# Hybrid GLA and differential-attention layer: an earlier split of the forget gate's weights, later stores of operand tiles, another spread of set units

## The chip, the cores and the metric

One core of a Trainium2 chip runs the kernel. The metric is the device time of one execution in microseconds; the time of a kernel is the median over its runs.

## The reference

One decoder layer over 256 tokens with 2048 features, in fp32. A normalised input goes through one wide projection; its columns feed two token mixers, whose outputs are merged by gates and projected once more:

```
h = rmsnorm(x, pre_norm_g);  proj = h @ w_in
a_q, a_k, a_v, a_g, a_lr, b_q, b_k, b_v, b_g, m_a, m_b = split(proj)
gk  = log_sigmoid(a_lr @ gla_gk_w2 + gla_gk_b) / 16          # forget gate
o_a = rmsnorm(gla_chunked(a_q, a_k, a_v, gk)) * silu(a_g);   y_a = o_a @ w_branch_a
o_b = rmsnorm(diff_attention(b_q, b_k, b_v, lam)) * (1 - lam_init) * silu(b_g)
y_b = o_b @ w_branch_b
merged = sigmoid(m_a) * y_a + sigmoid(m_b) * y_b
x = x + rmsnorm(merged @ w_out, post_norm_g)
```

`a_lr` has 16 columns, and `gla_gk_w2` is 16 x 1024. The weights are some 250 MB and are read once; the work is matmuls of 256 tokens against them.

## The kernel before

**Products.** Each fp32 product is made from rounded parts: a value is split into `hi` (a copy to the type fp32r) and `lo` (the rest), and hi x hi, hi x lo and lo x hi are summed. Weights come from DRAM in tiles of 128 x 2048 (1 MB, `raw`, three buffers). Half a tile is a *unit*. For each unit ACT copies it to `hi` (L297), DVE subtracts to get `lo` (L298), and PE multiplies (`token_major`, L457): eight matmuls of 512 columns with `hi`, four with `lo`. `hi` and `lo` have three buffers each, so ACT's copy for a step waits until PE is through with the step three before.

**Set units.** Five pairs of column groups (`SETS`) are computed by a scheme of seven products in place of eight. A product (p1, q3, p5, p2, q6, q7, p4) has four units; that makes 140 *set units*, six matmuls each (L656), whose `hi` and `lo` come from L258 and L259. Their weights are sums: tiles called `chain` are loaded by POOL DMAs (L212 plain, L210 with accumulation in the transfer); p2 needs a plain load `raw_s`, issued by SP (L252), which DVE also adds to a chain tile (L228). The other operand is a sum of parts of x, kept in tiles `square` (s1, n2, s4, n7, a hi and a lo each). They are made once; `store_squares` (called at L847, POOL DMAs at L620) writes all eight to DRAM, from where later sets read them back (`start_sets`, L632).

**Order.** `schedule()` writes the list of steps by hand: ordinary units by key, with set units put between. `mixed(n, *keys)` takes the next n set units and spreads them evenly over the units of these keys. The keys around the change are m12 and m13 (merge gates), y00 to y03 (first branch product: y_a in four groups of 512 columns, 8 units each) and y10 to y13 (second branch product), then o0 to o3. Loads and splits of a step are written down four steps before its matmuls. A scheduler then orders the instructions by priority and its own estimates, unless they are wrapped in `keep_in_program_order`; each engine runs its own list in order.

**Reads back.** The operands of the branch products, `oah` and `oal` for y0, `obh` and `obl` for y1, lie in DRAM and are read back by eight SP DMAs of 512 KB (`fetch`, L723, kept in program order), written down just ahead of y00 and of y10. SP also issues all loads of `raw` (L276), and a load waits on SP until its buffer is free.

**Forget gate.** Small jobs run in the background, one turn at a time, as generators that `pump()` steps. `forget_gate` transposes `lr` on PE (bank `bg`), splits it into `lrt`, splits `w2` into `w_s` (ACT L518, DVE L520) by way of `w2h` (ACT L519), and in its next turns multiplies them (PE L528).

Of the kernel before, what the change touches and what calls it, by code (L numbers as in the profile page):

```python
# [7 lines left out]
F32R = mybir.dt.float32r  # L8
BF16 = mybir.dt.bfloat16
U8 = mybir.dt.uint8  # L10
AF = mybir.ActivationFunctionType
ALU = mybir.AluOpType
AX = mybir.AxisListType

P = 128
# [15 lines left out]
def chunk_plan():  # L31

    plan = []
    at = 0
    for g, n in enumerate(VG):
        if g == 0:
            plan.append(("v0", "two", "w_in", [(6144, RANK), (2048, 2 * n - RANK)]))
            at = 2 * n - RANK
        elif g > 1:
            plan.append((f"v{g}", "tok", "w_in", [(2048 + at, n)]))  # L40
            at += n
    for hf in range(2):
        for name, base in (("k", 1024), ("q", 0)):
            for c in range(4):
                plan.append((f"{name}{hf}{c}", "chan", "w_in", [(base + 512 * hf + P * c, P)]))
    for g in range(4):
        plan.append((f"ag{g}", "tok", "w_in", [(4096 + 512 * g, 512)]))
    o = 6144 + RANK

    def heads(g):  # L50
        plan.append((f"dv{g}", "tok", "w_in", [(o + 4096 + 512 * g, 512)]))
        plan.append((f"bg{g}", "tok", "w_in", [(o + 6144 + 512 * g, 512)]))
        for pair in range(2):
            for n, name in enumerate(("dq", "dk")):
                for c in (2 * pair, 2 * pair + 1):
                    plan.append((f"{name}{g}{c}", "chan", "w_in", [(o + 2048 * n + 512 * g + P * c, P)]))

    def gate(br, g):
        plan.append((f"m{br}{g}", "tok", "w_in", [(o + 8192 + 2048 * br + 512 * g, 512)]))

    def branch(br, g):
        plan.append((f"y{br}{g}", "tok", ("w_branch_a", "w_branch_b")[br], [(512 * g, 512)]))

    for g in range(4):
        heads(g)
    for br, g in ((1, 2), (1, 3), (1, 0), (1, 1), (0, 0), (0, 1), (0, 2), (0, 3)):
        gate(br, g)
    for br in range(2):
        for g in range(4):
            branch(br, g)  # L70
    for g in range(4):
        plan.append((f"o{g}", "tok", "w_out", [(512 * g, 512)]))
    return plan


def units(kind):
    return 2 * KT // ROWS[kind]


def schedule():  # L80

    kinds = {key: kind for key, kind, _, _ in chunk_plan()}
    steps = []
    blocks = [(i, n) for i in range(len(SETS)) for n in range(SLOTS * 4)]

    def regular(*keys):
        steps.extend((key, n) for key in keys for n in range(units(kinds[key])))

    def mixed(n, *keys):
        at = len(steps)  # L90
        regular(*keys)
        r = steps[at:]
        del steps[at:]
        for i, step in enumerate(r):
            steps.extend(blocks[: (i + 1) * n // len(r) - i * n // len(r)])
            del blocks[: (i + 1) * n // len(r) - i * n // len(r)]
            steps.append(step)

    def channels(g):
        return [key for key in kinds if key[:2] in ("dq", "dk") and key[2] == str(g)]  # L100

    order = [key for key, _, _, _ in chunk_plan()]
    def alone(n):
        steps.extend(blocks[:n])
        del blocks[:n]

    regular(*order[: order.index("v4")])
    mixed(SLOTS * 4, *order[order.index("v4") : order.index("ag0")])
    regular(*order[order.index("ag0") : order.index("dq10")])
    mixed(18, *channels(1))  # L110
    mixed(18, *channels(2))
    mixed(18, *channels(3))
    mixed(16, "m12", "m13")
    mixed(32, *(f"y0{g}" for g in range(4)))
    mixed(10, "y10", "y11")
    regular("y12", "y13", *(f"o{g}" for g in range(4)))
    assert not blocks
    return steps
# [26 lines left out]
def hybrid_kernel(ctx: ExitStack, tc, xt, xn, preg, postg, w, w2, gkb, glag, lamv, diffg, ident_d, causal_d, lmask_d, out):  # L145
    nc = tc.nc
    pe, act, dve, pool, sp = nc.tensor, nc.scalar, nc.vector, nc.gpsimd, nc.sync
# [10 lines left out]
    def u(shape, name, dtype=F32):  # L158
        count[0] += 1
        return big.tile(shape, dtype, tag="u", name=f"{name}_{count[0]}")  # L160

    def sm(shape, name, dtype=F32, bufs=2):
        count[0] += 1
        return small.tile(shape, dtype, tag=name, name=f"{name}_{count[0]}", bufs=bufs)

    def t2(shape, name):
        count[0] += 1
        return small.tile(shape, F32, tag="t2", name=f"{name}_{count[0]}", bufs=8)

    def ps(tag):  # L170
        count[0] += 1
        return psum.tile([P, 512], F32, tag="bank", name=f"{tag}_{count[0]}")
# [5 lines left out]
    def f32(ap):  # L178
        return ap.bitcast(F32)


    steps = schedule()
    kinds, sizes, begins = {}, {}, {}
    off = 0
# [164 lines left out]
    w2_raw = u([P, 1024], "w2_raw")  # L349
    w2_s = u([P, 1024], "w2_s", F32R)  # L350
# [152 lines left out]
    act.activation(ones_r, ones, AF.Copy)  # L503

    def forget_gate():
        bank = ps("bg")
        for b in range(2):
            pe.transpose(bank[:, P * b : P * b + P], lr[:, b, :], ident)
        top = t2([P, 512], "lrh").bitcast(F32R)
        lrt = sm([P, S], "lrt", F32R, bufs=1)  # L510
        act.activation(top[:, :S], bank[:, :S], AF.Copy)
        for i in (0, 64):
            act.activation(lrt[i : i + 32, :], bank[i : i + 32, :S], AF.Copy)
            r = slice(i + 32, i + 64)
            dve.tensor_tensor(out=lrt[r, :], in0=bank[r, :S], in1=f32(top[r, :S]), op=ALU.subtract)
        top = u([P, 1024], "w2h", F32R)
        r = slice(64, P)
        act.activation(w2_s[:64, :], w2_raw[:64, :], AF.Copy)  # L518
        act.activation(top[r, :], w2_raw[r, :], AF.Copy)  # L519
        dve.tensor_tensor(out=w2_s[r, :], in0=w2_raw[r, :], in1=f32(top[r, :]), op=ALU.subtract)  # L520
        yield
        for hf in range(2):
            for c in range(2):
                bank = ps("bg")
                for i in range(2):
                    ct = 4 * hf + 2 * c + i
                    o = bank[:, S * i : S * i + S]
                    pe.matmul(o, w2_s[:, P * ct : P * ct + P], lrt, start=True, stop=True)  # L528
                for i in range(2):
                    ct = 4 * hf + 2 * c + i  # L530
                    act.activation(gp[hf][:, :, 2 * c + i, :], bank[:, S * i : S * i + S].rearrange("p (b t) -> p b t", b=2), AF.Identity, bias=gkb_s[:, ct : ct + 1])
            yield
        e = [u([P, 1024], "e") for _ in range(2)]
        z = [t.rearrange("p b c t -> p (b c t)") for t in gp]
        for hf in range(2):
            act.activation(e[hf], z[hf], AF.Abs)
            yield
            act.activation(e[hf], e[hf], AF.Exp, scale=-1.0)
            yield
        for hf in range(2):  # L540
            act.activation(e[hf], e[hf], AF.Ln, bias=1.0)
        for hf in range(2):
            yield
            dve.scalar_tensor_tensor(out=z[hf], in0=z[hf], scalar=0.0, in1=e[hf], op0=ALU.min, op1=ALU.subtract)
        done.add("gate")
# [71 lines left out]
    def store_squares():  # L617
        for name, far in parts_far.items():
            for t, src in zip(far, parts[name]):
                pool.dma_start(t, f32(src))  # L620

    def start_sets():
        n = started[0]
# [112 lines left out]
    tasks.append(late())  # L736
    tasks.append(operands)
    tasks.append(forget_gate())
    start = 2 * VG[0] - RANK
    for g, n in enumerate(VG[2:]):  # L740
# [92 lines left out]
    for hf in range(2):  # L833
        ts = {}
        for name in ("k", "q"):
            ts[name] = u([P, 2, 4, P], name)
            for c in range(4):
                o, o2 = (t.rearrange("p (b t) -> p b t", b=2) for t in channel_major(f"{name}{hf}{c}"))
                bc = rstd_bc.rearrange("p (b t) -> p b t", b=2)
                t = ts[name][:, :, c, :]  # L840
# [4 lines left out]
                pump(1)  # L845
        tasks.append(gla_scores(hf, ts["q"], ts["k"]))
    store_squares()  # L847


# [44 lines left out]
    for g in range(4):  # L894
# [6 lines left out]
        t = u([P, 2, 512], "ua")  # L901
# [207 lines left out]
    for g in range(4):  # L1109
        banks = token_major(f"y0{g}", 512, a_ops)  # L1110
        for b in range(2):
            t = t2([P, 512], "part")
# [49 lines left out]
    for g in range(4):  # L1162
# [8 lines left out]
        for b in range(2):  # L1171
            t = both[g][:, b, :]
# [9 lines left out]
    for b in range(2):  # L1182
        xres.append([])
        for i in range(2):
            t = u([P, 1024], "xres")
# [16 lines left out]
    def subtotal(b, parts):  # L1202
        r = sm([P, 1], "or", bufs=2)
        dve.tensor_reduce(out=r, in_=ssq[:, b, :parts], op=ALU.add, axis=AX.X)
        dve.tensor_scalar(out=r, in0=r, scalar1=1.0 / D, scalar2=EPS, op0=ALU.mult, op1=ALU.add)
        return r
# [30 lines left out]
    for c in range(2):  # L1237
# [6 lines left out]
        if c == 0:  # L1244
            square(1, bank[:, :256], 256, 3)
            gain(1, bank[:, :256], 1536, 256)
            r = subtotal(1, 4)
# [61 lines left out]
```

## Time and profile before

| | |
|---|---|
| runs | 1126.16 us median of 3 (1125.39 to 1126.97) |
| the profiled execution | 1127.69 us, its span 1125.9 us |
| mean granted TensorE clock | 0.994 |
| PE busy | 1108.4 us, 98% of the span, 5578 matmuls |
| DVE, ACT, POOL busy | 819.3, 679.9, 137.1 us |
| DMA | 274.56 MB, mean 244 GB/s |
| PE's longest waits | 3.5 us for `w_s` (L520), 2.0 us for a `lo` (L298) |

The span runs from the first to the last instruction. A timeline row has the start, the duration, engine and line, then output and inputs by the program's names; in brackets stands the idle time before it and what ended it. SPq is the queue of SyncE, which issues DMAs; how long a transfer took is read from its issue to its landing. A window row gives busy time and count of PE, PEld, DVE, ACT and POOL, then the granted clock, the share of the DMA engines and GB/s.

### The profile page before, as it was taken

The page shows a single profiled execution, that of the slowest core. Times are in us where ns is not written, and L with a number is a line of the kernel's source. Part 1 is how long each engine was busy: PE and PEld are TensorE (multiplying, and loading weights), DVE is VectorE, ACT ScalarE, POOL GpSimd, SP SyncE. Part 2 cuts the span into 40 slices and gives each one's busy share as a digit, 9 for nine tenths or more (in the row PEclk, how much of TensorE's full clock was granted, in tenths as well). Part 3 has the DMA queues.
Part 4 walks back from the last instruction along what each step waited for, and adds up shares of the span by engine and source line. Part 5 has one row for each costly group of instructions (what it writes and reads, how often), then busy time and mean ns, then how long its engine had stood idle before and what let it go on. Part 6 is the DMA issues. An engine that isn't in the chain of part 4 may idle for free. (4 is left out here: it accounts for less than half of the span.)

```text
span 1125.9 us, 15164 instructions
## 1 busy us (share of the span) xinstructions
PE 1108.4 (98%) x5578; PEld 954.0 (85%) x5578; DVE 819.3 (73%) x1151; ACT 679.9 (60%) x1004; POOL 137.1 (12%) x209
## 2 busy tenths in 40 slices
PE   9999999999999999999999999999999999999997
PEld 9989888888888888888888888888788888888886
DVE  6786769986677567658888878878676767585554
ACT  7767555654555457656777778775455555534451
POOL 0131100000001021212212312121112100000000
PEclk9998999999999999999999999999999999999999
DMA  8799764556565484989787989779889777588562
GB/s 310 263 375 351 231 186 157 208 185 248 179 257 208 166 310 167 393 208 249 227 277 215 242 254 243 229 216 261 333 300 256 200 300 247 180 342 309 188 211 75
DMA packets 55371, 274.56 MB, mean 244 GB/s; under 512 B 6848, under 2 KB 7488, under 8 KB 36608
## 3 DMA queue, kind: packets, MB, share of 16 engines
q1 hardware_dynamic: 33392, 195.97, 48.2%
q0 software_dynamic: 21184, 76.56, 25.4%
q10 hardware_dynamic: 720, 1.06, 0.3%
q8 instruction: 44, 0.72, 0.2%
q14 instruction: 31, 0.25, 0.1%
HBM read 249.44 MB, written 24.12 MB: 243 GB/s over the span
## 5 line engine op out<-in xcount | busy, mean ns | idle before, releaser
L457 PE MATMUL mm<-hi,xs 128*128 128x512 f32 (+2 forms) x896 | 216.8, 383 | 0.6 <-ACT hi L297 0.6
L478 PE MATMUL mm<-xs,hi 128*128 128x512 f32 x768 | 197.6, 391 | 0.0
L259 DVE TENSOR_TENSOR lo<-chain,hi 128x1024 fp32r<-128x1024 f32 x120 | 146.7, 1224 | 68.6 <-ACT hi L258 68.0
L258 ACT ACTIVATE hi<-chain 128x1024 fp32r<-128x1024 f32 x120 | 127.1, 1060 | 107.5 <-PE mm L457 46.7
L457 PEld LDWEIGHTS mm<-hi,xs 128*128 128x128 f32 x896 | 167.8, 190 | 25.8 <-ACT hi L297 1.1
L478 PEld LDWEIGHTS mm<-xs,hi 128*128 128x128 f32 x768 | 142.7, 188 | 27.3
L457 PE MATMUL mm<-lo,xs 128*128 128x512 f32 (+2 forms) x448 | 117.0, 380 | 0.0
L480 PEld LDWEIGHTS mm<-xs,lo 128*128 128x128 f32 x768 | 104.8, 190 | 7.5
L480 PE MATMUL mm<-xs,lo 128*128 128x256 f32 x768 | 107.1, 282 | 0.0
L298 DVE TENSOR_TENSOR lo<-raw_y,hi 128x1024 fp32r<-128x1024 f32 x64 | 78.1, 1223 | 37.5 <-ACT hi L297 37.3
L297 ACT ACTIVATE hi<-raw_y 128x1024 fp32r<-128x1024 f32 x64 | 67.7, 1062 | 57.1 <-PE mm L457 32.5
L457 PEld LDWEIGHTS mm<-lo,xs 128*128 128x128 f32 x448 | 84.7, 190 | 13.1 <-DVE lo L298 0.3
L656 PE MATMUL set<-hi,square 128*128 128x512 f32 x320 | 87.6, 396 | 0.0
L210 POOL DMA_DIRECT2D chain<-in_w_dram x56 | 48.8, 882 | 194.7 <-DVE lo L259 109.7
L656 PEld LDWEIGHTS set<-hi,square 128*128 128x128 f32 x320 | 58.7, 190 | 10.2
L656 PE MATMUL set<-hi,xs 128*128 128x512 f32 x240 | 65.6, 394 | 0.0
L297 ACT ACTIVATE hi<-raw_ag 128x1024 fp32r<-128x1024 f32 x32 | 33.9, 1061 | 39.9 <-PE mm L457 35.8
L298 DVE TENSOR_TENSOR lo<-raw_ag,hi 128x1024 fp32r<-128x1024 f32 x32 | 39.1, 1223 | 21.4 <-ACT hi L297 21.2
L457 PE MATMUL mm<-hi,obh 128*128 128x512 f32 x128 | 50.0, 391 | 0.8 <-ACT hi L297 0.8
L656 PEld LDWEIGHTS set<-hi,xs 128*128 128x128 f32 x240 | 43.8, 190 | 7.4
L298 DVE TENSOR_TENSOR lo<-raw_o,hi 128x1024 fp32r<-128x1024 f32 x25 | 30.6, 1225 | 26.8 <-ACT hi L297 26.6
L457 PE MATMUL mm<-hi,oah 128*128 128x512 f32 x128 | 49.9, 390 | 0.0
(273 smaller groups left out, 2069.0 us busy)
## 6 DMA issues: line engine op xcount, KB each, us to landing
chain<-in_w_dram POOLq DMA_DIRECT2D x96, 512.0 KB, 8.0
raw_y<-in_w_dram SPq DMA_DIRECT2D x32, 1024.0 KB, 6.3
raw_ag<-in_w_dram SPq DMA_DIRECT2D x16, 1024.0 KB, 4.8
raw_dq<-in_w_dram SPq DMA_DIRECT2D x16, 1024.0 KB, 5.4
raw_dk<-in_w_dram SPq DMA_DIRECT2D x16, 1024.0 KB, 7.4
raw_o<-in_w_dram SPq DMA_DIRECT2D x16, 1024.0 KB, 4.9
raw_v<-in_w_dram SPq DMA_DIRECT2D x15, 832.0 KB, 6.8
raw_s<-in_w_dram SPq DMA_DIRECT2D x10, 1024.0 KB, 8.2
```

The source lines that it names most:

```text
L210: pool.dma_start(dst, src, accum_op=ALU.add)
L258: act.activation(hi_t, raw, AF.Copy)
L259: dve.tensor_tensor(out=lo_t, in0=raw, in1=f32(hi_t), op=ALU.subtract)
L297: act.activation(hi_t[:, a:b], r, AF.Copy)
L298: dve.tensor_tensor(out=lo_t[:, a:b], in0=r, in1=f32(hi_t[:, a:b]), op=ALU.subtract)
L457: i = pe.matmul(banks[g][b][:, :n], a[part][:, P * b : P * b + P], w[:, c : c + n], start=first, stop=last)
L478: i = pe.matmul(o, hi[:, c], x_pair(kt), start=kt == 0, stop=kt == KT - 1)
L480: i = pe.matmul(o[:, :S], lo[:, c], x_ops(kt)[0], start=False, stop=False)
L656: i = pe.matmul(bank, a[part], wt[:, 512 * j : 512 * j + 512], start=go, stop=end, skip_group_check=not first)
```

## The change

1. `forget_gate`: the split of w2 goes ahead of the transposes and has a turn of its own.
2. `store_squares`: the eight stores are kept in program order, so behind what is written before them.
3. `schedule`: m12 and m13 take 14 set units (16 before); y00 takes 4 and y01 to y03 take 28 (the four groups shared 32); y10 and y11 take 12 (10).

```diff
@@ schedule
-    mixed(16, "m12", "m13")
-    mixed(32, *(f"y0{g}" for g in range(4)))
-    mixed(10, "y10", "y11")
+    mixed(14, "m12", "m13")
+    mixed(4, "y00")
+    mixed(28, *(f"y0{g}" for g in range(1, 4)))
+    mixed(12, "y10", "y11")
@@ forget_gate
     def forget_gate():
+        top = u([P, 1024], "w2h", F32R)
+        r = slice(64, P)
+        act.activation(w2_s[:64, :], w2_raw[:64, :], AF.Copy)
+        act.activation(top[r, :], w2_raw[r, :], AF.Copy)
+        dve.tensor_tensor(out=w2_s[r, :], in0=w2_raw[r, :], in1=f32(top[r, :]), op=ALU.subtract)
+        yield
         bank = ps("bg")
...
-        top = u([P, 1024], "w2h", F32R)
-        r = slice(64, P)
-        act.activation(w2_s[:64, :], w2_raw[:64, :], AF.Copy)
-        act.activation(top[r, :], w2_raw[r, :], AF.Copy)
-        dve.tensor_tensor(out=w2_s[r, :], in0=w2_raw[r, :], in1=f32(top[r, :]), op=ALU.subtract)
         yield
@@ store_squares
-                pool.dma_start(t, f32(src))
+                tc.keep_in_program_order(pool.dma_start(t, f32(src)))
```

In what follows y00.2 is unit 2 of the key y00, and p5.1 is unit 1 of product p5. Around the start of y00 the list of steps was: q3.3 m13.1 p5.0 m13.2 p5.1 m13.3 p5.2 m13.4 p5.3 m13.5 q6.0 m13.6 q6.1 m13.7 q6.2 y00.0 q6.3 y00.1 q7.0. It is now: q3.3 m13.3 p5.0 m13.4 p5.1 m13.5 p5.2 m13.6 p5.3 m13.7 y00.0 q6.0 y00.1 y00.2 q6.1 y00.3 y00.4 q6.2.

Three places in the engines' lists follow. First SP at the start of y00; a name like raw_y00_2 is the load of units 2 and 3 of y00, and oah and oal are the reads back. Before:

```order
L276 DMA raw_m13_6_7286<-in_w_dram 128x2048
L276 DMA raw_y00_0_7343<-in_w_dram 128x2048
L723 DMA oah_660_7393<-oah_far_184_2311 128x1024
L723 DMA oal_664_7397<-oal_far_188_2315 128x1024
L723 DMA oah_661_7394<-oah_far_185_2312 128x1024
L723 DMA oal_665_7398<-oal_far_189_2316 128x1024
```

After:

```order
L277 DMA raw_m13_6_7263<-in_w_dram 128x2048
L277 DMA raw_y00_0_7309<-in_w_dram 128x2048
L277 DMA raw_y00_2_7350<-in_w_dram 128x2048
L725 DMA oah_660_7374<-oah_far_184_2311 128x1024
L725 DMA oal_664_7378<-oal_far_188_2315 128x1024
L725 DMA oah_661_7375<-oah_far_185_2312 128x1024
```

raw_y00_2, which stood behind the eight reads back, now stands ahead of them. The load raw_s for p2 (raw_s3_20) stood between the loads raw_y00_4 and raw_y00_6 and now stands behind raw_y01_2. On PE the number of set matmuls ahead of the first matmul with oah goes from 594 to 576, which is three set units of six.

Second, SP at the start of y10, with obh and obl as the reads back. Before:

```order
L276 DMA raw_y10_0_8305<-in_w_dram 128x2048
L276 DMA raw_y10_2_8343<-in_w_dram 128x2048
L723 DMA obh_698_8367<-obh_far_244_3018 128x1024
L723 DMA obl_702_8371<-obl_far_248_3022 128x1024
L723 DMA obh_699_8368<-obh_far_245_3019 128x1024
```

After:

```order
L277 DMA raw_y10_0_8281<-in_w_dram 128x2048
L277 DMA raw_y10_2_8370<-in_w_dram 128x2048
L277 DMA raw_y10_4_8415<-in_w_dram 128x2048
L725 DMA obh_697_8344<-obh_far_244_3018 128x1024
L725 DMA obl_701_8348<-obl_far_248_3022 128x1024
```

raw_y10_4 has moved ahead of the reads back. Ahead of the first matmul with obh stand 768 set matmuls where 780 stood, two set units fewer. On PE the first two matmuls of y10.0 (with obh) are now followed by one set unit, and then by those with obl.

Third, ACT where w2 is split (w_s and w2h are the two copies; raw_v are weights of v4, chain_100 is the first set unit's tile; vh belongs to the value heads). Before:

```order
L297 ACTIVATE hi_910<-raw_v_0_908 128x800
L258 ACTIVATE hi_926<-chain_100_744 128x1024
L297 ACTIVATE hi_945<-raw_v_0_908 128x800
L518 ACTIVATE w_s_92<-w_raw_91 64x1024
L519 ACTIVATE w2h_804<-w_raw_91 64x1024
L555 ACTIVATE vh_120<-mm_580,rstd 128x208
```

After:

```order
L298 ACTIVATE hi_900<-raw_v_0_898 128x800
L259 ACTIVATE hi_916<-chain_100_744 128x1024
L298 ACTIVATE hi_942<-raw_v_0_898 128x800
L509 ACTIVATE w_s_92<-w_raw_91 64x1024
L510 ACTIVATE w2h_794<-w_raw_91 64x1024
L557 ACTIVATE vh_120<-mm_580,rstd 128x208
```

Here nothing has changed places: the same three copies stand ahead of the split and the same vh behind it. The eight stores of the squares, on POOL, stood among the loads of the first chain tiles and now stand behind the gate store gate_far_48, ahead of the second MEMSET of `suf`.

## The prediction

> **What bounds the kernel now.** I read the page first, then the list of PE's waits, then the timeline of each engine around the two longest waits and around the place where the order changes.
>
> ```profile
> span 1125.9 us, 15164 instructions
> PE 1108.4 (98%) x5578; PEld 954.0 (85%) x5578; DVE 819.3 (73%) x1151; ACT 679.9 (60%) x1004; POOL 137.1 (12%) x209
> ```
>
> PE is busy for 98% of the span, and the change leaves the matmuls as they are. So time can come only from PE's waits and from matmuls that run at a lower clock. The waits, by the line that is waited for (total, times, longest):
>
> ```profile
> PE bg L528 <- DVE w_s L520: 3.5, 1, 3.5
> PE mm L457 <- DVE lo L298: 2.0, 1, 2.0
> PE mm L457 <- ACT hi L297: 1.4, 2, 0.8
> ```
>
> The first two are the targets of the change; I call them A and B. Both cost more than the wait. For B, PE's timeline (start, duration, what it did, in brackets the wait before it) and a window with the granted clock (PEclk, the third number from the end):
>
> ```profile
> 807.94 1.66 PE L457 MATMUL mm<-lo,oah 128*128 128x512 f32 x4 [1.95 <-DVE lo L298]
> ...
> 811.91 0.40 PE L457 MATMUL mm<-hi,oah 128*128 128x512 f32 x1
> ...
> 813.77 1.08 PE L457 MATMUL mm<-lo,oah 128*128 128x512 f32 x4
> ...
> 816.05 0.39 PE L457 MATMUL mm<-hi,oah 128*128 128x512 f32 x1
> ```
>
> ```profile
> 808.00:810.00 2.00, 2.00 (x6) 1.58 (x7) 2.00 (x2) 1.02 (x1) 0.00 (x0) 0.61 0.57 119
> ```
>
> The ten matmuls from 807.94 to 811.91 took 3.97 us; the same ten from 813.77 to 816.05 took 2.28. The clock was 0.61, so the wait of 1.95 cost another 1.69: B costs 3.64. For A, ACT and PE:
>
> ```profile
> 81.22 0.87 ACT L297 ACTIVATE hi<-raw_v 128x800 fp32r<-128x800 f32 x1 [0.98 <-PE mm L457]
> 82.00 1.04 ACT L518 ACTIVATE w_s<-w_raw 64x1024 fp32r<-64x1024 f32 x1
> ```
>
> ```profile
> 85.42 2.08 PE L528 MATMUL bg<-lrt,w_s 128*128 128x256 f32 x8 [3.48 <-DVE w_s L520]
> ...
> 92.85 1.61 PE L457 MATMUL mm<-hi,xs 128*128 128x400 f32 x8
> ...
> 96.42 0.91 PE L457 MATMUL mm<-hi,xs 128*128 128x400 f32 x4
> ```
>
> From 85.42 to 92.85 is 7.43 us: the eight gate matmuls of 256 columns, one unit of v4 and one set unit. The next such pair, without gate matmuls, takes 3.57. Eight of 256 columns are about 0.9, an estimate from half of the 1.81 between the starts of eight of 512 and what follows them below. So about 2.9 is lost clock, and A costs 6.4.
>
> **Part 1, the split of w2: 0.** In the code it comes a turn sooner; in ACT's order it does not. The two copies stand behind the same three rows as before, the last of them the copy at 81.22, which waited for PE (the buffer of the last v3 unit). ACT works in order, so L518 starts at 82.00 again, DVE's L520 follows, and PE's gate matmuls keep their place. What does move (transposes and the split of lr) waits for nothing here. A stays; the other end is that all of it goes, −6.4.
>
> **Part 2, the stores of the operand tiles: 0.** Eight POOL transfers go from among the first chain loads to behind the last gate store.
>
> ```profile
> 238.94 0.54 POOL L712 DMA_DIRECT2D gate_far<-mgate  x1 [19.17 <-ACT mgate L711]
> 272.98 0.95 POOL L772 MEMSET suf<- 128x1024 f32 x1 [33.50 <-DVE att L768]
> L297 ACT ACTIVATE hi<-raw_ag 128x1024 fp32r<-128x1024 f32 x32 | 33.9, 1061 | 39.9 <-PE mm L457 35.8
> ```
>
> ```profile
> 262.18 0.37 SPq L723 DMA_DIRECT2D vh<-vh_far  x1
> ```
>
> POOL was idle for 33.50 us there, which covers eight issues. The later reads of these tiles come hundreds of us behind. What the stores can hold is the tiles' buffers, which SP's fetches of vh and vl take from 262.18, ahead of the ag weights: these weights' copies waited 35.8 us in all for PE, about 1.1 each, and that is the cover; without it the cost is that of a short wait, up to B's 3.64. At the start the chain loads come sooner, yet ACT's copy at 81.22 waits for PE and not for a load, so nothing is won either. I take 0, between −1 and +1.
>
> **Part 3, the counts: B goes, C and D come.** A set unit is 1.36 us of PE (790.33 to 791.69 below), an ordinary unit 2.72. Three set units fewer now stand ahead of y00.0: PE reaches it 4.08 sooner. Rows of DVE, SP, PE, then what a transfer took to land:
>
> ```profile
> 776.80 1.22 DVE L298 TENSOR_TENSOR lo<-raw_m,hi 128x1024 fp32r<-128x1024 f32 x1
> ```
>
> ```profile
> 770.02 0.33 SPq L276 DMA_DIRECT2D raw_y<-in_w_dram  x1
> 770.44 0.38 SPq L723 DMA_DIRECT2D oah<-oah_far  x1
> 770.99 0.33 SPq L723 DMA_DIRECT2D oal<-oal_far  x1
> ...
> 794.07 0.33 SPq L252 DMA_DIRECT2D raw_s<-in_w_dram  x1
> ```
>
> ```profile
> 779.45 1.98 PE L457 MATMUL mm<-hi,xs 128*128 128x512 f32 x8
> 781.26 1.07 PE L457 MATMUL mm<-lo,xs 128*128 128x512 f32 x4
> ...
> 790.33 1.07 PE L656 MATMUL set<-hi,square 128*128 128x512 f32 x4
> ...
> 791.69 0.39 PE L457 MATMUL mm<-hi,oah 128*128 128x512 f32 x1
> ```
>
> ```profile
> oah<-oah_far SPq DMA_DIRECT2D x1, 512.0 KB, 13.7
> ```
>
> ```profile
> oal<-oal_far SPq DMA_DIRECT2D x1, 512.0 KB, 17.0
> ```
>
> *B goes (−3.64).* raw_s was issued at 794.07, behind all of the fetch burst, and its add on DVE held the lo that PE waited for. In after it is due a group later (y01), when the burst is over; I price its new slack at nothing (it stands behind one more load on SP; the other end is B again, a rival).
>
> *C comes at y00.0 (+8.4).* Before, the eight fetches followed raw_y00_0. Now raw_y00_2 stands ahead of them, and it takes the buffer of m13's units 4 and 5: it waits for DVE's lo of m13.5, the row at 776.80, end 778.02, 1.43 before PE's start on that unit at 779.45. In after m13.5 has two set units fewer ahead of it: PE starts it at 776.73, the lo ends at 775.30, and SP issues raw_y00_2 at 775.33, 5.31 later than raw_y00_0. Queued behind it, in SP's order, are the eight fetches: oah 0.42 later (775.75), the first oal 0.97 later (776.30). At 13.7 and 17.0 us they land at 789.45 and 793.30. PE wants the first at 791.69 − 4.08 = 787.61: it waits 1.84, does one matmul (0.23) and waits 3.6 for oal: 5.45 idle. A fetch takes that long here for what shares the queue:
>
> ```profile
> 770.00:788.00 18.00, 18.00 (x81) 14.92 (x80) 13.31 (x11) 9.91 (x11) 1.78 (x3) 1.00 0.99 285
> 788.00:806.00 18.00, 17.98 (x79) 14.40 (x78) 8.47 (x8) 10.22 (x12) 2.76 (x5) 1.00 1.00 400
> ```
>
> From 770 to 788 the engines are full at 285 GB/s (the last number), with four accumulating chain loads from POOL among the transfers; without them, 400. In after those loads follow the same set units and shift with them. For the lost clock the nearest rows are B (1.69 after 1.95) and A (2.9 after 3.48); C idles longer than both, so 2.9. C is 5.5 to 8.4; I take 8.4.
>
> The Trainium skill ("TensorE: Matmul & The Clock Gate", Part 1: The HAM clock gate) says that the clock halves after at least one idle window of about 3.4 us and is whole again after as much sustained work. By it only the second half of C would cost clock, about 1.7, and D none: the sum would be +5.1. The row at 808 speaks against it: 1.95 us of idle time already brought the clock to 0.61.
>
> *D comes at y10.0 (+3.2).* Two set units fewer stand ahead of it in all; the fetches of obh move behind raw_y10_4.
>
> ```profile
> 912.36 0.42 SPq L723 DMA_DIRECT2D obh<-obh_far  x1
> 912.84 0.42 SPq L723 DMA_DIRECT2D obl<-obl_far  x1
> ```
>
> ```profile
> obh<-obh_far SPq DMA_DIRECT2D x1, 512.0 KB, 5.8
> ```
>
> ```profile
> obl<-obl_far SPq DMA_DIRECT2D x1, 512.0 KB, 6.6
> ```
>
> ```profile
> 918.95 1.23 DVE L298 TENSOR_TENSOR lo<-raw_y,hi 128x1024 fp32r<-128x1024 f32 x1 [0.60 <-ACT hi L297]
> ```
>
> ```profile
> 922.13 0.39 PE L457 MATMUL mm<-hi,oah 128*128 128x512 f32 x1
> ...
> 924.85 0.39 PE L457 MATMUL mm<-hi,obh 128*128 128x512 f32 x1
> ```
>
> raw_y10_4 takes y03's last buffer, free when the lo of y03.7 ends: 920.18, which is 1.95 before PE's start on that unit (922.13). Counted from that start, SP issues raw_y10_4 at −1.92 and obh at −1.54; obh lands at +4.26 and is wanted at +2.72 (924.85): 1.54 idle. obl lands at +5.54, and PE, busy with a set unit, wants it later. Clock on top: 0 (two waits of 0.8 in the list) or 1.69 (B). 1.54 is nearest to 1.95, so D is 3.2, from 1.5.
>
> **The sum.** 1127.69 (the profiled execution) − 3.64 + 8.4 + 3.2 = 1135.65. That execution is 1.53 above the median of the runs, 1126.16, so the median after is 1134.1. With the low ends of C and D, 1129.5; the case's own range is 1129 to 1135.5.
>
> **Rivals.**
> *The fetches land in time (0.18).* If the burst at y00 goes at the pace of the burst at y10 (5.8 and 6.6), oal lands at 782.9, 4.7 before it is wanted, and C is nil. It decides at 11.5 us from issue to landing for the first oal: below that no wait. For it: fewer set units ahead may leave fewer accumulating loads in the queue. Against: 17.0 in the trace, and the loads shift along. Then −3.64 + 1.5 (D without lost clock) gives 1124.0; with D between 0 and 3.2, 1122.5 to 1125.7: not slower. The Trainium skill ("DMA: Bandwidth & Descriptors", Queues, rings and completion order) has each DMA engine take turns between queues by packet, so SP's transfers would get half of the rate and land in time; 0.5 MB from 784.1 (oah) to 788.0 (oal) is 136 GB/s, a third of what the second window moved.
> *The split does run sooner (0.04).* A goes too: 1134.1 − 6.4 = 1127.7. Against it, ACT's order.
> *raw_s is late again, at y01 (0.10).* It stands behind raw_y01_2 on SP, waits for that load's buffer, and B's 3.64 comes back: 1137.7.
> *C is half (0.08).* The landing is 3 to 4 us quicker, so that only one wait of about 2 is left, with B's lost clock: 3.6 in place of 8.4, 1129.3.
>
> **How the numbers follow.** The forecast has 0.60. The range of 1124.0 to 1138.0 holds it, the half C, the late raw_s, the split, and the slower part of the first rival (D at 1.5 or more). 0.2%, about what a measurement of this kernel can tell from no change, is 2.25 us: faster is under 1123.9, slower over 1128.4. Faster: two thirds of the first rival, 0.12. Same: the rest of it 0.06, the split 0.04, and a quarter of the half C 0.02, so 0.12. Slower: 0.76.
>
> **What would show it.** In the profile after: the wait of PE for w_s still there with about 3.5; no wait for the lo of raw_y near y01; a new wait of PE for a DMA (oah, then oal) at y00.0, 1.8 and 3.6; one of about 1.5 for obh at y10.0; PEclk near 0.5 to 0.6 in the 3 to 6 us behind each. SP issues raw_y00_2 straight ahead of the fetches, about 5 us later than raw_y00_0 was. I am wrong if oal lands within 11.5 us, if the wait for w_s is gone, or if PE waits where this text names nothing.

## The result and the profile after

The changed kernel takes 1131.83 us, median of 6 runs (1129.74 to 1135.86); the kernel before, run beside it and counted with its first runs, 1125.67 (1125.14 to 1126.97, 6 runs). The ratio is 1.0057 with a 95% interval of 1.0038 to 1.0077: slower by 6.2 us. The forecast was 1134.1.

The changed kernel's profiled execution took 1131.25 us, its span is 1129.5. PE's waits on the page of waits (line waited for: total, times, longest):

```profile
PE bg L530 <- DVE w_s L511: 3.5, 1, 3.5
PE mm L458 <- DMA oal<-oal_far: 2.9, 1, 2.9
PE mm L458 <- DMA obh<-obh_far: 2.3, 1, 2.3
PE mm L458 <- ACT hi L298: 2.0, 3, 0.8
PE bg L966 <- DVE prob L961: 1.8, 2, 1.3
```

The first line is A, unchanged. B, the wait for a `lo`, is gone from the list. The second and third are C and D, which were not there before. The last, for `prob`, had 0.5 in the profile before; its longest lies between 400 and 560 us, far from the new counts.

At y00.0, SP's queue (start, duration of the issue), two landing times of its reads and PE's timeline:

```profile
766.75 9.10 SPq L277 DMA_DIRECT2D raw_y<-in_w_dram  x2
775.95 0.40 SPq L725 DMA_DIRECT2D oah<-oah_far  x1
776.52 1.03 SPq L725 DMA_DIRECT2D oal<-oal_far  x1
```

```profile
oah<-oah_far SPq DMA_DIRECT2D x1, 512.0 KB, 11.3
```

```profile
oal<-oal_far SPq DMA_DIRECT2D x1, 512.0 KB, 14.6
```

```profile
787.80 0.39 PE L458 MATMUL mm<-hi,oah 128*128 128x512 f32 x1
791.12 0.50 PE L458 MATMUL mm<-hi,oal 128*128 128x512 f32 x1 [2.93 <-DMA oal<-oal_far]
...
796.71 0.39 PE L458 MATMUL mm<-hi,oah 128*128 128x512 f32 x1
```

SP issued raw_y00_0 at 766.75 and then stood until 775.85 before it got rid of raw_y00_2; the reads came right behind it. The first oal was issued at 776.52 and landed 14.6 us later, at 791.1. PE wanted it at 788.03. From 787.80 to 796.71, one unit of y00 and one set unit took 8.91 us where 2.72 + 1.36 = 4.08 is usual, so C cost 4.8 here. Of this, 2.93 is idle time and about 1.9 is lost clock (PEclk 0.50 in this window):

```profile
792.00:794.00 2.00, 2.00 (x6) 1.57 (x5) 0.00 (x0) 0.02 (x1) 0.00 (x0) 0.50 1.03 422
```

At y10.0, SP's queue and PE's timeline:

```profile
901.39 18.33 SPq L277 DMA_DIRECT2D raw_y<-in_w_dram  x3
919.77 0.42 SPq L725 DMA_DIRECT2D obh<-obh_far  x1
```

```profile
922.28 1.07 PE L458 MATMUL mm<-lo,oah 128*128 128x512 f32 x4
925.63 0.70 PE L458 MATMUL mm<-hi,obh 128*128 128x512 f32 x2 [2.28 <-DMA obh<-obh_far]
```

The third load is raw_y10_4; obh stood behind it on SP and PE waited 2.28. The clock behind the wait is full (the 1.00):

```profile
926.00:928.00 2.00, 2.00 (x10) 1.63 (x9) 0.00 (x0) 0.71 (x1) 0.00 (x0) 1.00 1.02 369
```

So D is the idle time and little more in this execution, some 2.5.

At A, the same wait as before, and then less time lost to the clock:

```profile
84.93 1.87 PE L530 MATMUL bg<-lrt,w_s 128*128 128x256 f32 x8 [3.48 <-DVE w_s L511]
...
91.09 1.64 PE L458 MATMUL mm<-hi,xs 128*128 128x400 f32 x8
```

From the gate matmuls to the second unit of v4 it took 6.16 us, where the same instructions took 7.43 in the profile before. The two spans differ by 3.6. The pieces come close to it: −3.64 (B) − 1.27 (A's clock) + 4.8 (C) + 2.5 (D) + 1.3 (longer waits for prob) = 3.7. Smaller changes are left out, such as PE's waits for `hi` in the first 10 us (0.6 before, 1.1 after).

### The profile page after: what moved, and what is told of

It is laid out like the page before. It is cut to its first block, busy times and chain, and to the rows that moved or that the text cites. A ratio compares the mean times of both kernels' runs of the same rounds, so it can differ in the third digit from the quotient of the medians.

```text
span 1129.5 us, 15167 instructions
## 1 busy us (share of the span) xinstructions
PE 1106.8 (98%) x5578; PEld 951.7 (84%) x5578; DVE 818.6 (72%) x1151; ACT 680.0 (60%) x1004; POOL 136.7 (12%) x209
## 4 chain that ended last, share of the span: by engine, by line
PE 92%; DMA 2%; issue 2%; ACT 1%; DVE 1%; POOL 0%; SPq 0%; DVEq 0%; POOLq 0%; ACTq 0%
PE mm L458 45%; PE set L658 16%; PE mm L479 15%; PE mm L481 8%; PE bg L458 2%; DMA oal<-oal_far 1%; PE bg L812 1%; PE mm L441 1%; PE bg L441 1%; PE bg L940 1%; PE bg L941 1%; DMA raw_v<-in_w_dram 1%; DMA obh<-obh_far 1%; PE bg L966 0%; ACT hi L298 0%
## 5 line engine op out<-in xcount | busy, mean ns | idle before, releaser
L458 PE MATMUL mm<-hi,oal 128*128 128x512 f32 x128 | 50.6, 395 | 2.9 <-DMA oal<-oal_far 2.9
```

The source lines that it names most:

```text
L458: i = pe.matmul(banks[g][b][:, :n], a[part][:, P * b : P * b + P], w[:, c : c + n], start=first, stop=last)
```

## The experiments

Each kernel was run five rounds against the kernel before. "Changed" below is the changed kernel, 1131.83. The kernel before had medians of 1125.82 beside E1 to E4, 1125.57 beside E5 to E8 and 1126.25 beside E9 and E10. The changed kernel was not run again beside them, so a difference from it is one between sessions. All waits are from the runs' own profiles.

**E1: parts 1 and 2 alone.**

```diff
-    mixed(14, "m12", "m13")
-    mixed(4, "y00")
-    mixed(28, *(f"y0{g}" for g in range(1, 4)))
-    mixed(12, "y10", "y11")
+    mixed(16, "m12", "m13")
+    mixed(32, *(f"y0{g}" for g in range(4)))
+    mixed(10, "y10", "y11")
```

> The changed kernel with the counts of before (16, 32, 10): parts 1 and 2 alone, the early split and the later stores. Theory (the slowdown is part 3's, from the reads back that stand behind one more weight load on SP): the same as before, within 1 us of 1125.7, the wait for w_s still 3.5, B back with about 2. Rival (the later stores or the moved transposes cost time at the start): 2 us or more above before.

Measured 1125.35, ratio 0.999 (0.9979 to 1.0002): the same as before. Its profile is of the fastest of its 12 executions, 1122.12. The wait for w_s is there in full, and in this execution it costs nothing beyond itself:

```profile
84.68 1.22 PE L529 MATMUL bg<-lrt,w_s 128*128 128x256 f32 x8 [3.48 <-DVE w_s L510]
...
89.30 1.64 PE L457 MATMUL mm<-hi,xs 128*128 128x400 f32 x8
```

That stretch is 4.62 here, against 6.16 and 7.43 above, for the same 3.48 of idle time. B is only 0.88 here:

```profile
803.61 1.20 PE L457 MATMUL mm<-lo,oah 128*128 128x512 f32 x4 [0.88 <-DVE lo L298]
```

**E2: part 3 alone**, the kernel before with the new counts (E1's diff the other way).

> The kernel before with the new counts alone. Theory: all of the slowdown, 5 to 6.5 us above before, with a wait for oal of about 3 at y00.0 and one for obh of about 2.3 at y10.0. Rival (parts 1 and 2 carry some of it): under 4 us above before.

Measured 1133.20, ratio 1.0065 (1.0052 to 1.0078), with waits of 1.1 for oah, 3.3 for oal and 2.2 for obh. At +7.4 it lies a little above the 5 to 6.5 expected. Its interval overlaps with the changed kernel's, and E1 has no slowdown: it is part 3's.

**E3: the reads back ahead of raw_y00_2 again.**

```diff
     mixed(4, "y00")
+    i = steps.index(("y00", 2))
+    steps[i], steps[i + 1] = steps[i + 1], steps[i]
```

> The changed kernel with one pair of steps exchanged in y00: the set unit q6.1 now stands ahead of y00.2, so that raw_y00_2 is written down behind the eight reads back and SP issues oah straight behind raw_y00_0. The number of set units ahead of y00.0 stays as in the changed kernel. Theory (C comes from the load that SP must wait for): the wait for oal goes to under 1 us, and the time is 4 to 6 us under that of the changed kernel, 1126 to 1128. Rival (C comes from PE's arrival 4.08 us sooner while the transfers are slow): a wait for oah or oal of 2 us or more stays, and the time is within 1.5 us of the changed kernel's.

Measured 1133.81, ratio 1.0066 (1.0054 to 1.0078). No wait for oah or oal is left, so they were indeed late because of the load ahead of them. Yet nothing was won. SP's queue, the landing of raw_y00_2, and PE at y00.2:

```profile
767.62 0.33 SPq L279 DMA_DIRECT2D raw_y<-in_w_dram  x1
768.05 0.60 SPq L727 DMA_DIRECT2D oah<-oah_far  x1
...
776.39 26.98 SPq L279 DMA_DIRECT2D raw_y<-in_w_dram  x4
```

```profile
raw_y<-in_w_dram SPq DMA_DIRECT2D x1, 1024.0 KB, 23.1
```

```profile
800.68 0.50 PE L460 MATMUL mm<-hi,oah 128*128 128x512 f32 x1 [3.69 <-ACT hi L300]
```

raw_y00_2 was issued at 776.39, took 23.1 us behind the eight reads, and ACT's copy, and with it PE, waited for it: 3.69, longer than the wait it replaced. Neither theory of this experiment holds. The order on SP only chooses which transfer is late. The new theory, stated in E5's expectation, was that there are too many bytes for the rate at that place.

**E4: D alone taken away.**

```diff
-    mixed(28, *(f"y0{g}" for g in range(1, 4)))
-    mixed(12, "y10", "y11")
+    mixed(30, *(f"y0{g}" for g in range(1, 4)))
+    mixed(10, "y10", "y11")
```

> The changed kernel with 10 set units in y10 and y11 as before, and 30 in y01 to y03; raw_y10_4 stands behind the reads of obh again. Theory: the wait for obh goes, C stays as it is, and the time is 2 to 3 us under that of the changed kernel. Rival (obh waits for its buffers and not for the load ahead of it): a wait for obh of about 2 stays, no change.

Measured 1129.71, ratio 1.0031 (1.002 to 1.0041): 2.1 under the changed kernel. The two intervals just overlap, so this size is uncertain; the profile is clearer. obh was issued at 915.23, with raw_y10_4 behind it, and the wait for it is gone; those for oah (1.3) and oal (3.3) are there. D is the load ahead of the reads, as predicted.

**E5: plain loads in place of accumulating ones.**

```diff
             dve.tensor_tensor(out=x, in0=x, in1=y, op=ALU.add)
-            late(n, "q7", unit)
+            late(n, "q7", unit, add=n != 3)
```

> The changed kernel with the four loads of set 3 that add to a chain tile behind p5 (for q7) made plain ones; it leaves these four sums out. They are in flight while oah and oal are read back. E3 showed that with the reads ahead the next weight load is late instead, so C is now taken for a matter of amount: too many bytes for the rate at that place. Theory (the accumulating loads hold the rate down): the rate from 770 to 788 us rises from 236 GB/s to 350 or more, oal lands within 11 us, the wait for oal is under 0.5, and the time is 4 to 6 us under that of the changed kernel. Rival (the bytes alone are too many at any rate): a wait for oal of 2 us or more stays, and the time is within 1.5 us of the changed kernel's.

It leaves four sums out, so only its time is of use. Measured 1126.75, ratio 1.0011 (1.0002 to 1.002): 5.1 under the changed kernel. There is no wait for oah or oal. The window from 770 to 788 us, in the changed kernel and then in E5 (last number GB/s, ahead of it the share of DMA time that is busy):

```profile
770.00:788.00 18.00, 18.00 (x81) 14.73 (x79) 15.09 (x13) 9.89 (x10) 3.47 (x4) 1.00 0.92 236
```

```profile
770.00:788.00 18.00, 18.00 (x81) 14.92 (x80) 14.90 (x14) 10.10 (x11) 2.17 (x4) 1.00 0.84 310
```

The first oal, behind raw_y00_2 as in the changed kernel, was issued at 776.28 and landed sooner:

```profile
oal<-oal_far SPq DMA_DIRECT2D x1, 512.0 KB, 8.9
```

The rate was 310 and not the 350 expected, but with a smaller busy share: the transfers were through earlier and the engines had pauses. With four loads of the same half megabyte each, issued within 0.3 us of the same times, that read took 8.9 us in place of 14.6 when they did not accumulate. The DMA queues from 768 to 792 us show what they took (queue, packets, MB, share of the 16 engines' time; POOL's loads are in q0, SP's in q1). The changed kernel:

```profile
q0 software_dynamic: 615, 2.19, 51.5%
q1 hardware_dynamic: 763, 3.85, 43.5%
```

E5:

```profile
q1 hardware_dynamic: 1273, 5.71, 60.7%
q0 software_dynamic: 604, 2.15, 27.8%
```

For about the same bytes q0 held the engines almost twice as long while four of its loads accumulated, and SP's queue got 3.85 MB through where it got 5.71 in E5.

**E6: the split of w2 put ahead in ACT's and DVE's order**, with the counts of before.

```diff
+            if (key, unit) == ("v4", 0):
+                with tc.issue_after(split[0]):
+                    act.activation(hi_t[:, a:b], r, AF.Copy)
+                with tc.issue_after(split[1]):
+                    dve.tensor_tensor(out=lo_t[:, a:b], in0=r, in1=f32(hi_t[:, a:b]), op=ALU.subtract)
+                continue
...
-        act.activation(top[r, :], w2_raw[r, :], AF.Copy)
-        dve.tensor_tensor(out=w2_s[r, :], in0=w2_raw[r, :], in1=f32(top[r, :]), op=ALU.subtract)
+        split.append(act.activation(top[r, :], w2_raw[r, :], AF.Copy).ins)
+        split.append(dve.tensor_tensor(out=w2_s[r, :], in0=w2_raw[r, :], in1=f32(top[r, :]), op=ALU.subtract).ins)
```

> The counts of before, parts 1 and 2 of the change, and an order put on ACT and DVE so that v4's first copy and its lo stand behind the split of w2: the split then does run sooner on the engines. Theory (A is ACT's order): no wait for w_s over 0.5, a new one of at most 1 us for v4's copies, and 3 to 5 us under before. Rival (the copies of v4 that are held back are as late as w_s was): a wait for hi or lo of 2.5 us or more at the same place, and a time within 1.5 us of before.

Measured 1119.81, ratio 0.995 (0.9937 to 0.9962): 5.8 under before, a little more than the 3 to 5 expected, and no new wait came up at v4. ACT's timeline has w2h ahead of v4's first copy, and PE goes through:

```profile
75.52 1.06 ACT L517 ACTIVATE w2h<-w_raw 64x1024 fp32r<-64x1024 f32 x1
76.60 0.76 ACT L564 ACTIVATE vh<-mm,rstd 128x208 fp32r<-128x208 f32 x2
77.25 0.87 ACT L301 ACTIVATE hi<-raw_v 128x800 fp32r<-128x800 f32 x1
```

```profile
80.95 1.07 PE L537 MATMUL bg<-lrt,w_s 128*128 128x256 f32 x8
81.86 1.62 PE L465 MATMUL mm<-hi,xs 128*128 128x400 f32 x8
```

The second copy starts 7.1 us sooner than in the changed kernel (82.57), where the scheduler had left it behind copies that wait for PE. B is still there, with 1.96.

**E7: the reads of oah and oal sooner**, the rest as in the changed kernel.

```diff
+    oah, oal = [], []
     for g in (2, 3):
+        if g == 3:
+            for i in range(4):
+                for t, name, far in ((oah, "oah", oah_far), (oal, "oal", oal_far)):
+                    t.append(u([P, 2, 2, S], name, F32R))
+                    fetch(f32(t[i]), far[i])
         banks = token_major(f"m1{g}", 512, x_ops, 2)
...
-    oah = [u([P, 2, 2, S], "oah", F32R) for _ in range(4)]
-    oal = [u([P, 2, 2, S], "oal", F32R) for _ in range(4)]
-    for i in range(4):
-        fetch(f32(oah[i]), oah_far[i])
-        fetch(f32(oal[i]), oal_far[i])
```

> The changed kernel with the eight reads of oah and oal written down before m13 instead of before y00; SP issues them behind raw_m13_6, some 10 us sooner, where the DMA engines are under half busy (0.42 to 0.46 from 750 to 768 us). Order of the steps and counts as in the changed kernel. Theory (amount at that place): neither oal nor raw_y00_2 is late, no wait over 0.5 us near y00, and the time is 4 to 6 us under the changed kernel's, with D and A as they are. Rival (the reads hold up another load or wait for their buffers until the same time): a wait of 2 us or more near y00 stays.

Measured 1126.40, ratio 1.0009 (0.9999 to 1.0019): 5.4 under the changed kernel. The reads start at 756.08, and nothing near y00 waits for them or for raw_y00_2; the same bytes, moved twenty microseconds earlier, cost nothing:

```profile
755.64 0.33 SPq L277 DMA_DIRECT2D raw_m<-in_w_dram  x1
756.08 0.37 SPq L725 DMA_DIRECT2D oah<-oah_far  x1
```

```profile
oal<-oal_far SPq DMA_DIRECT2D x1, 512.0 KB, 7.0
```

**E8 and E10: all four taken away**, E6's order, E7's reads and E4's counts in one kernel, run twice.

> E6's order for the split, E7's sooner reads, and the new counts with 10 instead of 12 set units in y10 and y11 (30 in y01 to y03): A, B, C and D all taken away. Theory: their prices add up, so 1117 to 1120. Rival (what is taken away at one place comes back as a wait at the next): 1122 or more.

> E8 once more, beside E9 on the same chip: 1118 to 1120, and no wait over 1.5 us in its profile.

Measured 1118.77, ratio 0.9937 (0.9924 to 0.9949), and 1117.91, ratio 0.9933 (0.992 to 0.9945). The second lies just under the 1118 expected. What is left of waits is short; the longest are 1.3 and 1.2 for prob. The prices add up: 1125.57 less 5.8 (A, by E6) and some 1.3 (B, worked out below) is 1118.5.

**E9: the same with the counts of before.**

> E8 with the counts of before (16, 32, 10): the early split and the sooner reads alone. It tells what part 3's counts are worth once C and D are away. If they are worth B's measured wait and clock (2 to 3.6 us), this kernel is 2 us or more slower than E8 run beside it; if the sooner reads take B away as well (raw_s no longer stands in a crowd), it is within 1 us of E8.

Measured 1117.07 (1116.44 to 1118.05), ratio 0.9924 (0.9911 to 0.9938), beside E10's 1117.91. The intervals overlap. So once the reads are sooner, no gain from E8's counts can be seen, and B has gone with the crowd: the wait for a `lo` is missing from E9's list as well. This is the lowest median of the kernels tried, 9.2 under the kernel before it ran beside.

## Why the prediction was right, point by point

**A stays: right.** The wait is 3.48 in both profiles, because ACT's order did not move. Its price of 6.4 was that of one execution: the same 3.48 cost 2.8 us of clock in the profile before (7.43 against 4.62), 1.5 after, and nothing in E1. E6 makes A worth 5.8 by the medians.

**Part 2 is free: right**, as far as E1 tells: parts 1 and 2 together cost −2.4 to +0.2 us by its interval.

**B goes: right, but 3.64 was probably too much.** That was again one execution: B was 1.95 with 1.69 of clock in the profile before, 0.88 in E1, 1.96 without lost clock in E6. By the medians, E7 keeps D (2.1 by E4) and has no B and no C, and is 0.8 over before, so B was worth some 1.3. Two other pairs spread around this: E6 has B, and E8, which has not, is 1.0 under it; E9, which is E6 with the sooner reads, is 3.4 further under its kernel before than E6 was. Together these put B between 1 and 3.4.

**C comes: right in place, too large in size.** The term was 8.4, the top of its 5.5 to 8.4; it measured 4.8 in the profile and 5.4 by E7's median. The same stretch cost 6.5 in E2's profile and 7.9 in E4's, so 8.4 fits a slow execution (E4's profile is of the slowest of its nine) and not the median. The step that failed is the landing time carried over from the profile before: oah took 11.3 and not 13.7, so that PE did not wait for it here (in E2 and E4 it did, for 1.1 and 1.3), and oal 14.6 and not 17.0, so that 2.93 were idle and not 5.45. Why they landed 2.4 us sooner is not shown. The lost clock was 1.9 for 2.9. This is halfway to the rival "C is half": a landing 2.4 us quicker and one wait, of 2.93 for its 2. SP's times were close: raw_y00_2 gone by 775.85, and oal issued at 776.52, against 775.33 and 776.30. The prediction put the late issue down to the load ahead of the reads, and the slow landing to the accumulating loads among them. Both were borne out. What it did not see is that the order alone decides nothing here: E3 mended it, and the next load was late. E5 and E7 showed what helps: the bytes fit when the accumulating loads become plain, or when the reads start while the engines have room.

**D comes: right.** It was 2.5 for 3.2: the idle time 2.28 for 1.54, since the `lo` that frees the buffer ended only 1.1 ahead of PE's unit and not 1.95, and no clock was lost. The 1.69 of clock that the prediction put on top was lost in other executions, 1.7 each in the profiles of E3 and E7.

The first rival named 11.5 us for the first oal as the point below which nothing waits; 14.6 in the changed kernel and 8.9 in E5 lie on the sides it gave. (In E7 the reads start 20 us sooner, so its 7.0 does not test the point.) The longer waits for prob are named nowhere in the prediction; E1, without the new counts, has one of 1.1 too, and no run was made for them.

The forecast slowdown was 8.0 and the measured one 6.2, inside an interval of 4.3 to 8.7. Part of that closeness is luck: B's gain and C's cost were both priced from single executions and both came out too large, and the two errors have opposite signs.

## What to carry to other kernels

Where DMA engines are full for a stretch, as here behind 770 us, changing which transfer goes first may only choose who waits; look at the window ahead of the stretch for room, and start there what is known early. A piece of code moved up in the program can move nothing while a scheduler orders by other rules: read the engine's list, and if the row has not moved, the wait has not either. Price a short wait of PE by several profiles, since the clock that it costs differs from one to the next.

## What the runs showed of the hardware that was not expected

The clock lost after one and the same wait of 3.48 us was 0, 1.5 or 2.8 us in three profiles (E1, the changed kernel, the kernel before). Waits of about 2 us cost either nothing or 1.7: B cost 1.69 in the profile before (1.95 idle) and nothing in E6 (1.96); D cost nothing in the changed kernel (2.28) and in E5 (2.41), and 1.7 in E3 (2.26) and E7 (2.24). The window behind D in E7 has a granted clock of 0.50:

```profile
922.00:924.00 2.00, 2.00 (x7) 1.52 (x6) 0.00 (x0) 0.68 (x1) 0.00 (x0) 0.50 1.04 324
```

The Trainium skill ("TensorE: Matmul & The Clock Gate", Part 1: The HAM clock gate) says that the activity window runs freely, so that the same kernel changes clock at different points; that fits this spread. Its idle window of about 3.4 us does not explain the 1.69 lost after 1.95. What sets the loss in a given run is left open; no run here was made for it.

A load that adds into its destination held back the other transfers more than a plain load of the same size: with four such loads the first oal took 14.6 us to land, with four plain ones 8.9. The queue that carries them took 51.5% of the engines' time for 2.19 MB with them and 27.8% for 2.15 MB without. What inside a transfer takes that time is not shown.
